# Prompt attention of a hybrid decoder layer: 64-query halves with 192 keys each, on parts of the TensorE array

## The chip, the core and the metric

The kernel runs on one core of one Trainium2 chip. The core has a matrix engine (TensorE, PE in the profile; its weight loads are listed apart as PEld), VectorE (DVE), ScalarE (ACT), GpSimd (POOL) and SyncE (SP), which here issues most transfers. Matrix products leave TensorE through PSUM, which has eight banks of 128 partitions by 512 fp32 values; DVE and ACT read them from there into SBUF, the working memory. The metric is device time of one execution in microseconds (us), as the median of several runs.

## What is computed

One decoder layer for a prompt of 1024 tokens and 8 sample sequences of 8 tokens: a gated feed-forward half step, a mixer, and a second feed-forward half step. The mixer has two head groups side by side: windowed attention and a gated linear recurrence (HGRN2). The change is in the attention of the prompt alone. It has 8 query heads of 64 columns, two key heads (each serves four query heads), a window of 128 tokens, and one learned sink per head that takes part in the softmax:

```python
s = jnp.einsum('bnqhgd,bnkhd->bnhgqk', qb, kk) * SCALE     # blocks of 128 queries, 256 keys
dist = qi + W - kj
band = (dist >= 0) & (dist <= WINDOW)
...
m = jnp.maximum(jnp.max(s, axis=-1, keepdims=True), sk)
p = jnp.exp(s - m)
den = jnp.sum(p, axis=-1, keepdims=True) + jnp.exp(sk - m)
...
out = jnp.einsum('bnhgqk,bnkhd->bnqhgd', p, vv)
```

A block of 128 queries sees the 128 keys before it and its own 128. A query sees at most 129 of these 256, so about half of each score matrix is masked. The first 64 queries of a block see only keys 0 to 191 of its 256, the last 64 only keys 64 to 255.

## The kernel before

**Stages and order.** The 1024 prompt tokens and 64 sample tokens go through in three groups of 320, 384 and 384 columns (n = 0, 1, 2), with 2, 3 and 3 prompt blocks of 128 queries; group 0 also has the sample tokens. Dense products of the feed-forward and projection layers are made by `mm3` (L249 to L253): each weight is split into a high and a low part, and three products (high by high, high by low, low by high) are added in one bank. These three lines are most of what TensorE does. The mixer is written as Python generators. `mixer(n)` (L1528) runs two chains in turn through `both`: one with `intra` and `hgrn_block`, one with `attn_block`. Each `yield` ends a step; `tick()` between dense products lets a stream go on by a rate given per group (`RM`, 0.97, 0.92 and 1.2 steps a tick). So the small products of the attention are strewn among dense ones. `need("m2")` (L1688) and the like run what is left of a stream at once.

A planner then walks the traced instructions with a simulated clock. It gives each tile a free buffer of its tag and puts the instructions of each engine in an order of its own: an instruction that is not ready there is overtaken by later ones that are. Each engine runs its list strictly in that order. Tags that matter here: `ax` (L65), four PSUM banks shared by all small products, and `t2` (L279), eight SBUF buffers of 512 columns. The dense products have four banks of their own.

**The attention of one block** (`attn_block`, L1185). Two passes, `pr` = 0 and 1, take four heads each: `g` is the key head, `i` the head within the pass.

- *Scores* (L1202): for each `i` and `g`, one product of 64 rows (the head's columns; key head `g` lies on partitions 64g to 64g+63) by 128 queries, with 256 keys streamed through. Each `g` writes its own bank. In the first block of the prompt there are 128 keys.
- *Softmax* (L1210 to L1222): DVE adds the mask `amask` and takes the row maximum in one instruction per head; small instructions merge it with the sink; ACT takes the exponential with a row sum per head. Two yields follow.
- *Transposes* (L1230): per `g` a bank with four 128 by 128 transposes of probabilities, then a copy to SBUF (L1233), by DVE for g = 0 and ACT for g = 1. One yield.
- *Values* (L1241): for each of two key blocks and each `g`, one product of 128 keys by 64 value columns, with 256 columns (two heads of 128 queries) streamed. Both `g` go to one bank `ob`, on its two halves of partitions, and this bank is kept over both passes. The scores of the second pass follow without a yield.
- After both passes: one copy of `ob` to SBUF (L1248), four transposes (`pvT`, L1252), division by the row sum, `finish_attn`.

A product of fp32 operands shows as two matmul records in the trace, a transpose as one.

`mix_consts` (L145) makes `amask` once, while the first feed-forward runs: a memset and two selections on GpSimd give a 128 by 256 band.

## Time and profile before

| quantity | value |
|---|---|
| median of 3 runs | 1960.29 us (1959.91 to 1961.1) |
| profiled execution, its own time | 1960.04 us |
| its span, first to last instruction | 1958.3 us |
| granted TensorE clock, mean | 0.999 |
| PE busy | 1945.1 us |
| DVE, ACT, POOL busy | 1431.4, 948.3, 171.9 us |
| transfers | 375.23 MB, mean 192 GB/s |

The span is that of the profiled execution; its own time has 1.7 us more around the span. Busy times of matmuls overlap: a matmul record lasts from its issue to its modelled end, and the next starts long before that. What a group of matmuls takes is therefore read from the starts: from its first start to the start of what follows on the same engine. In the groups, a form such as 64*128 stands for the rows and columns of the array that a product occupies; the shape behind it is the streamed operand. The prompt attention lies between 724 and 1304 us of the span.

### The profile page before, as it was taken

Reading aid. Unit: us, or ns where it says so; the run is one execution under the profiler, and the core shown is the slowest. Engines: PE = TensorE matmul, PEld = TensorE weight load, DVE = VectorE, ACT = ScalarE, POOL = GpSimd, SP = SyncE. Lnnn points to the kernel's source line nnn. Section 1 sums busy time; section 2 is a strip of 40 time slices with the busy share of each in tenths; the row PEclk is TensorE's granted clock in tenths of the full one; section 3 lists DMA queues with packets and bytes.
Section 4 is the critical chain, followed back from the end, with each engine's and each line's share of the span. In section 5 each row is a group of like instructions: output and inputs, shape, how many; then the busy total and the mean of one; then the engine's idle time right before and its main releaser. Section 6 shows DMA issues by size and latency. Waiting matters only on the chain.

```text
span 1958.3 us, 33735 instructions
## 1 busy us (share of the span) xinstructions
PE 1945.1 (99%) x13071; PEld 1817.2 (93%) x13071; DVE 1431.4 (73%) x2471; ACT 948.3 (48%) x1689; POOL 171.9 (9%) x161
## 2 busy tenths in 40 slices
PE   9999999999999999999999999999999999999998
PEld 9999999999998988778999898989999999999887
DVE  6896789886567656777677757756987887656666
ACT  5553444444445444435345545765644444445453
POOL 1300000000003102111121303000000000000202
PEclk9999999999999999999999999999999999999999
DMA  6643667655667547764424344536555645677974
GB/s 246 208 139 121 226 232 262 222 193 186 233 229 235 177 137 247 258 206 150 119 90 151 98 136 131 162 123 222 167 203 197 211 171 190 212 237 230 309 258 141
DMA packets 175601, 375.23 MB, mean 192 GB/s; under 512 B 16128, under 2 KB 67520, under 8 KB 175424
## 3 DMA queue, kind: packets, MB, share of 16 engines
q1 hardware_dynamic: 169536, 362.58, 55.2%
q10 hardware_dynamic: 5904, 10.49, 1.6%
q8 instruction: 102, 1.67, 0.3%
q14 instruction: 59, 0.48, 0.1%
HBM read 290.60 MB, written 83.39 MB: 191 GB/s over the span
## 4 chain that ended last, share of the span: by engine, by line
PE 91%; DVE 3%; DMA 3%; issue 1%; POOL 1%; ACT 1%; SPq 0%; DVEq 0%; POOLq 0%; ACTq 0%
PE mm L251 27%; PE mm L252 27%; PE mm L253 27%; DMA raw<-in_ffn_w_gu_dram 1%; PE sc L1202 1%; PE pv L1241 1%; PE pT L1230 1%; PE lv L1288 1%; DVE w L232 1%; DMA fa<-big 0%; PE c L253 0%; PE c L251 0%; PE c L252 0%; DVE t L751 0%; PE av L1375 0%
## 5 line engine op out<-in xcount | busy, mean ns | idle before, releaser
L251 PE MATMUL mm<-h,wsph 128*128 128x320 f32 (+1 forms) x1344 | 428.4, 320 | 0.0
L252 PE MATMUL mm<-h,wsph 128*128 128x320 f32 (+1 forms) x1344 | 425.6, 317 | 0.0
L253 PE MATMUL mm<-h,wspl 128*128 128x320 f32 (+1 forms) x1344 | 423.3, 316 | 0.0
L232 DVE TENSOR_TENSOR wspl<-raw,wsph 128x1024 fp32r<-128x1024 f32 x208 | 259.8, 1249 | 131.5 <-ACT wsph L231 130.1
L231 ACT CAST wsph<-raw 128x1024 fp32r<-128x1024 f32 x208 | 217.9, 1049 | 272.2 <-PE mm L252 215.1
L251 PEld LDWEIGHTS mm<-h,wsph 128*128 128x128 f32 x1344 | 252.3, 188 | 8.6 <-issue 6.7
L252 PEld LDWEIGHTS mm<-h,wsph 128*128 128x128 f32 x1344 | 252.6, 188 | 4.6 <-issue 3.8
L253 PEld LDWEIGHTS mm<-h,wspl 128*128 128x128 f32 x1344 | 252.0, 188 | 0.7 <-issue 0.4
L231 ACT CAST w<-raw 128x512 fp32r<-128x512 f32 (+1 forms) x208 | 153.8, 745 | 200.3 <-PE mm L252 90.0
L251 PE MATMUL mm<-h,w 128*128 128x384 f32 (+1 forms) x736 | 246.4, 335 | 1.0 <-ACT big L802 0.6
L252 PE MATMUL mm<-h,w 128*128 128x384 f32 (+1 forms) x736 | 245.9, 334 | 0.0
L253 PE MATMUL mm<-h,w 128*128 128x384 f32 (+1 forms) x736 | 240.6, 334 | 0.4 <-POOL w L604 0.4
L232 DVE TENSOR_TENSOR w<-raw,w 128x512 fp32r<-128x512 f32 (+1 forms) x208 | 178.3, 862 | 71.9 <-ACT w L231 71.2
L252 PE MATMUL mm<-w,h 128*128 128x512 f32 x462 | 180.8, 391 | 0.5 <-DVE w L232 0.5
L251 PE MATMUL mm<-w,h 128*128 128x512 f32 x462 | 180.3, 393 | 0.0
L253 PE MATMUL mm<-w,h 128*128 128x512 f32 x462 | 180.2, 392 | 0.0
L251 PE MATMUL mm<-big,w 128*128 128x384 f32 x528 | 176.7, 335 | 0.1
L252 PE MATMUL mm<-big,w 128*128 128x384 f32 x528 | 176.6, 334 | 0.0
L253 PE MATMUL mm<-big,w 128*128 128x384 f32 x528 | 176.0, 334 | 0.0
L251 PEld LDWEIGHTS mm<-h,w 128*128 128x128 f32 x736 | 138.3, 188 | 2.3 <-ACT big L802 1.3
L252 PEld LDWEIGHTS mm<-h,w 128*128 128x128 f32 x736 | 138.2, 188 | 0.4 <-DVE h L613 0.2
L253 PEld LDWEIGHTS mm<-h,w 128*128 128x128 f32 x736 | 137.8, 188 | 0.9 <-POOL w L604 0.6
(338 smaller groups left out, 3380.6 us busy)
## 6 DMA issues: line engine op xcount, KB each, us to landing
raw<-in_ffn_w_gu_dram SPq DMA_DIRECT2D x162, 512.0 KB
raw<-in_ffn_w_down_dram SPq DMA_DIRECT2D x74, 512.0 KB
raw<-in_w_in_dram SPq DMA_DIRECT2D x54, 512.0 KB
ar<-fa SPq DMA_DIRECT2D x70, 384.0 KB
big<-in_ffn_w_down_dram SPq DMA_DIRECT2D x88, 256.0 KB
fb<-big SPq DMA_DIRECT2D x44, 512.0 KB
fa<-big SPq DMA_DIRECT2D x22, 768.0 KB
raw<-fb SPq DMA_DIRECT2D x30, 512.0 KB
```

The costliest lines, as they stand in the source:

```text
L231: made['S'] = S.copy(hi, src).ins
L232: (lo_eng or V).tensor_tensor(lo, src, hi.bitcast(F32), op=ALU.subtract)
L251: PE.matmul(out, a[0], b[0], start=first, stop=False, skip_group_check=resume)
L252: PE.matmul(out, a[0], b[1], start=False, stop=False, skip_group_check=resume)
L253: return PE.matmul(out, a[1], b[0], start=False, stop=last, skip_group_check=resume).ins
L1202: PE.matmul(banks[g][:, i * 256:i * 256 + wk], zq[64 * g:64 * g + 64, 2 * pr + i, b * P:(b + 1) * P], kx[64 * g:64 * g + 64, k0:k0 + wk], ...
L1230: PE.transpose(bank[:, (kb * 2 + i) * P:(kb * 2 + i + 1) * P], pt[g][:, i, kb * P:(kb + 1) * P], ident)
L1241: PE.matmul(ob[64 * g:64 * g + 64, pr * 256:pr * 256 + 256], vn[:, vb, 64 * g:64 * g + 64], pT[g][:, kb * 256:kb * 256 + 256], start=kb == ...
L1288: PE.matmul(b5[32 * i:32 * i + 32, b, a], K[:, a, cs], Q[:, a, cs], start=True, stop=True)
```

## The change

The block of 128 queries is cut into two halves `hq` of 64 queries with 192 keys each.

- *Mask*: `amask` becomes 128 by 192. The band is made in a temporary tile; the upper half of the partitions copies its columns 0 to 191, the lower half columns 64 to 255.
- *Scores*: eight products per pass in place of four, each 64 rows by 64 columns of the array, with 192 keys streamed. `g` chooses the rows of the array, `hq` the columns. Queries of half `hq` land on partitions 64 hq to 64 hq + 63.
- *Softmax*: the same instructions over 192 columns. In the first block, where the halves have 64 and 128 keys, each instruction becomes two.
- *Probability tile*: it takes the middle 384 columns of a 512-column tile, and GpSimd zeroes 64 by 64 values at two corners (two memsets per `g`), so that every transpose can read 128 columns.
- *Transposes*: sixteen per pass in place of eight, each of 64 queries by 128 columns, on one 64-row half of the array; half `hq` writes its own bank. Still two copies of 512 columns, now one for each `hq`.
- *Values*: twelve products per pass in place of four, each 64 keys by 64 value columns, with 128 columns streamed. The row half of the array (`par`) chooses one of two banks; the order of work is three turns of four products.
- *Eviction of the values*: per pass, ACT copies one bank to SBUF and DVE adds the other, in place of one copy per block. The SBUF tile `of_` is taken at the start of the block.

```diff
--- before.py
+++ after.py
@@ -39,6 +39,7 @@
 LEVELS = [64, 32, 16, 8, 4, 2, 1]
 NRAW = 3
 WARM = 12
+PLACE = ((0, 0, 1), (1, 0, 0))
 P1 = 1.0
 
 
@@ -128,7 +129,7 @@
     f1pre = cp.tile([P, KC], F32, name="f1pre")
     halfpost = cp.tile([P, 16], F32, name="halfpost")
     sinkb = cp.tile([P, 8], F32, name="sinkb")
-    amask = cp.tile([P, 256], F32, name="amask")
+    amask = cp.tile([P, 192], F32, name="amask")
     smask = cp.tile([P, 136], F32, name="smask")
     ssink = cp.tile([P, 2], F32, name="ssink")
     seqm = cp.tile([NS, 4], F32, name="seqm")
@@ -146,11 +147,14 @@
         nc.sync.dma_start(sinkb, A["attn_sinks"].partition_broadcast(P))
         nc.sync.dma_start(ssink, A["sample_sinks"])
 
-        V.memset(amask, 0.0)
-        G.affine_select(amask, amask, pattern=[[1, 256]], compare_op=ALU.is_ge, fill=NEG,
+        band = tmp2("band", (P, 256))
+        V.memset(band, 0.0)
+        G.affine_select(band, band, pattern=[[1, 256]], compare_op=ALU.is_ge, fill=NEG,
                         base=0, channel_multiplier=-1)
-        G.affine_select(amask, amask, pattern=[[-1, 256]], compare_op=ALU.is_ge, fill=NEG,
+        G.affine_select(band, band, pattern=[[-1, 256]], compare_op=ALU.is_ge, fill=NEG,
                         base=P, channel_multiplier=1)
+        V.tensor_copy(amask[0:64], band[0:64, 0:192])
+        V.tensor_copy(amask[64:P], band[64:P, 64:256])
         tmp = pp.tile([P, 8, P], I32, tag="big", bufs=12, name="mtmp")
         tf = pp.tile([P, 8, P], F32, tag="big", bufs=12, name="mtmpf")
         col, row, x = tmp[:, 0], tmp[:, 1], tmp[:, 2]
         def attn_block(n, b):
             zq, kx, vn = Z[n]["q"], KX[n], VN[n]
             first = n == 0 and b == 0
-            nk = 1 if first else 2
-            k0 = P if first else b * P
-            wk = nk * P
-            mask = amask[:, P:] if first else amask
             sm, mx = small(), small()
-            ob = None
+            of_ = t2()
+            halves = (0, 1)
 
             def of(x, pr):
                 return x.rearrange("p (g r i) -> p g r i", g=2, r=2)[:, :, pr]
 
+            def cols_of(hq):
+                return slice((128, 64)[hq] if first else 0, 192)
+
+            def rows(par):
+                return slice(64 * par, 64 * par + 64)
+
             for pr in range(2):
-                pt, banks = [], [axbank("sc") for _ in range(2)]
+                pt, banks = [], [axbank("sc")[:, :384].rearrange("p (i c) -> p i c", i=2) for _ in range(2)]
                 for i in range(2):
-                    for g in range(2):
-                        PE.matmul(banks[g][:, i * 256:i * 256 + wk],
-                                  zq[64 * g:64 * g + 64, 2 * pr + i, b * P:(b + 1) * P],
-                                  kx[64 * g:64 * g + 64, k0:k0 + wk], start=True, stop=True)
+                    for hq in halves:
+                        cs = cols_of(hq)
+                        k0 = b * P + 64 * hq
+                        for g in range(2):
+                            PE.matmul(banks[g][rows(hq), i, cs],
+                                      zq[rows(g), 2 * pr + i, b * P + 64 * hq:b * P + 64 * hq + 64],
+                                      kx[rows(g), k0 + cs.start:k0 + cs.stop], start=True, stop=True)
+                parts = [(rows(hq), cols_of(hq)) for hq in halves] if first else [(slice(0, P), slice(0, 192))]
                 for g in range(2):
-                    p = t2((P, 2, 256))
-                    pt.append(p)
+                    pad = t2()
+                    p = pad[:, 64:448].rearrange("p (i c) -> p i c", i=2)
+                    pt.append((p, pad))
+                    G.memset(pad[rows(0), 448:], 0.0)
+                    G.memset(pad[rows(1), :64], 0.0)
                     for i in range(2):
                         hd = 4 * g + 2 * pr + i
-                        V.tensor_tensor_reduce(out=p[:, i, :wk], in0=banks[g][:, i * 256:i * 256 + wk], in1=mask,
-                                               op0=ALU.add, op1=ALU.max, scale=1.0, scalar=NEG,
-                                               accum_out=mx[:, 0, hd:hd + 1])
+                        for rs, cs in parts:
+                            V.tensor_tensor_reduce(out=p[rs, i, cs], in0=banks[g][rs, i, cs], in1=amask[rs, cs],
+                                                   op0=ALU.add, op1=ALU.max, scale=1.0, scalar=NEG,
+                                                   accum_out=mx[rs, 0, hd:hd + 1])
                 V.scalar_tensor_tensor(of(sm[:, 0], pr), of(mx[:, 0], pr), 0.125, of(sinkb, pr),
                                        op0=ALU.mult, op1=ALU.max)
                 V.tensor_scalar(of(sm[:, 1], pr), of(sm[:, 0], pr), -1.0, None, op0=ALU.mult)
                 for g in range(2):
                     for i in range(2):
                         hd = 4 * g + 2 * pr + i
-                        S.activation(pt[g][:, i, :wk], pt[g][:, i, :wk], AF.Exp, bias=sm[:, 1, hd:hd + 1],
-                                     scale=0.125, accum_out=mx[:, 1, hd:hd + 1])
+                        for rs, cs in parts:
+                            S.activation(pt[g][0][rs, i, cs], pt[g][0][rs, i, cs], AF.Exp, bias=sm[rs, 1, hd:hd + 1],
+                                         scale=0.125, accum_out=mx[rs, 1, hd:hd + 1])
                 V.tensor_tensor(of(sm[:, 2], pr), of(sinkb, pr), of(sm[:, 0], pr), op=ALU.subtract)
                 S.activation(of(sm[:, 2], pr), of(sm[:, 2], pr), AF.Exp)
                 yield
                 yield
-                pT = []
+                pT, tb2 = [], [axbank("pT").rearrange("p (g i s q) -> p g i s q", g=2, i=2, s=2) for _ in range(2)]
                 for g in range(2):
-                    bank = axbank("pT")
-                    for kb in range(nk):
-                        for i in range(2):
-                            PE.transpose(bank[:, (kb * 2 + i) * P:(kb * 2 + i + 1) * P],
-                                         pt[g][:, i, kb * P:(kb + 1) * P], ident)
-                    t = t2()
-                    (S.copy if g else V.tensor_copy)(t[:, :2 * wk], bank[:, :2 * wk])
+                    for i in range(2):
+                        for slot, at in ((0, (0, 64)), (1, (128, -64))):
+                            for hq in halves:
+                                if not first or at[hq] >= cols_of(hq).start:
+                                    c = 64 + 192 * i + at[hq]
+                                    PE.transpose(tb2[hq][:, g, i, slot], pt[g][1][rows(hq), c:c + P],
+                                                 ident[rows(hq), rows(hq)])
+                for hq in halves:
+                    t = t2((P, 2, 2, 2, 64))
+                    ss = slice(1 - hq, 2 - hq) if first else slice(0, 2)
+                    (S.copy if hq else V.tensor_copy)(t[:, :, :, ss], tb2[hq][:, :, :, ss])
                     pT.append(t)
                 yield
-                if ob is None:
-                    ob = axbank("pv")
-                for kb in range(nk):
-                    vb = b + kb + (1 if first else 0)
+                ob = [axbank("pv")[:, :256].rearrange("p (i h q) -> p i h q", i=2, h=2) for _ in range(2)]
+                for turn in (((0, 0), (0, 1)), ((0, 2), (1, 0)), ((1, 1), (1, 2))):
                     for g in range(2):
-                        PE.matmul(ob[64 * g:64 * g + 64, pr * 256:pr * 256 + 256], vn[:, vb, 64 * g:64 * g + 64],
-                                  pT[g][:, kb * 256:kb * 256 + 256], start=kb == 0, stop=kb == nk - 1)
+                        for par, (hq, blk) in enumerate(turn):
+                            if 64 * blk >= cols_of(hq).start:
+                                alone = (hq, blk) in ((0, 1), (1, 1))
+                                PE.matmul(ob[par][rows(g), :, hq], vn[rows(par), b + (blk + hq) // 2, rows(g)],
+                                          pT[hq][rows(par), g, :, PLACE[hq][blk]],
+                                          start=alone or first or blk == 0, stop=alone or blk == 2)
+                src = of_[:, pr * 256:pr * 256 + 256].rearrange("p (i h q) -> p i h q", i=2, h=2)
+                if first:
+                    S.copy(src[:, :, 0], ob[0][:, :, 0])
+                    V.tensor_copy(src[:, :, 1], ob[0][:, :, 1])
+                    V.tensor_tensor(src[:, :, 1], ob[1][:, :, 1], src[:, :, 1], op=ALU.add)
+                else:
+                    S.copy(src, ob[0])
+                    V.tensor_tensor(src, ob[1], src, op=ALU.add)
                 if pr:
                     yield
             V.tensor_tensor(mx[:, 2], mx[:, 1], sm[:, 2], op=ALU.add)
             V.reciprocal(mx[:, 3], mx[:, 2])
-            of_ = t2()
-            S.copy(of_, ob)
             yield
             tb = axbank("pvT")
             for m in range(4):
```

## Prediction

> **What bounds the kernel now.** I read the engine totals and the chain of waits first, then the groups by form, then the timeline of TensorE around single groups.
>
> ```profile
> PE 1945.1 (99%) x13071; PEld 1817.2 (93%) x13071; DVE 1431.4 (73%) x2471; ACT 948.3 (48%) x1689; POOL 171.9 (9%) x161
> ...
> PE 91%; DVE 3%; DMA 3%; issue 1%; POOL 1%; ACT 1%; SPq 0%; DVEq 0%; POOLq 0%; ACTq 0%
> ```
>
> TensorE is never free for long and 91% of the chain lies on it. A microsecond of its queue saved is therefore about a microsecond of the end, as long as no new wait on it appears. The three groups of prompt attention, by form:
>
> ```profile
> L1202 PE MATMUL sc<-kx,big 64*128 64x256 f32 x112 | 21.8, 404 | 0.0
> L1241 PE MATMUL pv<-t,vn 128*64 128x256 f32 x120 | 19.7, 395 | 0.0
> L1230 PE MATMUL pT<-ident,t 128*128 128x128 f32 x120 | 18.5, 276 | 0.8 <-ACT t L1219 0.8
> ```
>
> There are 16 passes (8 blocks, 2 each), 14 of them with 256 keys. Eight score records, eight value records and eight transposes make a pass. Busy times overlap, so what a pass takes is read from starts:
>
> ```profile
> 1290.16 0.31 PE L253 MATMUL mm<-h,wspl 128*128 128x320 f32 x1
> 1290.40 0.65 PE L1241 MATMUL pv<-t,vn 128*64 128x256 f32 x2
> 1290.97 1.14 PE L1202 MATMUL sc<-kx,big 64*128 64x256 f32 x8
> 1292.04 1.08 PE L1241 MATMUL pv<-t,vn 128*64 128x256 f32 x6
> 1293.05 0.41 PE L251 MATMUL mm<-h,wsph 128*128 128x320 f32 x1
> 1293.30 0.31 PE L252 MATMUL mm<-h,wsph 128*128 128x320 f32 x1
> ...
> 724.33 0.72 PE L1202 MATMUL sc<-kx,big 64*128 64x128 f32 x8
> 724.97 0.50 PE L251 MATMUL mm<-w,h 128*128 128x512 f32 x1
> ```
>
> Eight score records take 1.07 us with 256 keys (1290.97 to 1292.04) and 0.64 with 128. Two records run at once, one per key head: eight records are four rounds. So 128 streamed columns cost (1.07 - 0.64)/4 = 0.105 us a round, 256 cost 0.21, and 0.22 of the 1.07 is fixed: the first weight load, not hidden, and a gap after. Two value records (one product alone, two rounds) take 0.57, so their fixed part is 0.15.
>
> A stay of TensorE in a form other than 128*128 also delays the dense products on either side. The best row is an isolated stay of transposes in half the array, in the sample tokens:
>
> ```profile
> 903.93 0.33 PE L252 MATMUL mm<-h,wsph 128*128 128x384 f32 x1
> 904.10 0.34 PE L253 MATMUL mm<-h,wspl 128*128 128x384 f32 x1
> 904.37 0.46 PE L1350 MATMUL hT<-ident,t 64*128 64x64 f32 x4
> 904.76 0.45 PE L251 MATMUL mm<-h,wsph 128*128 128x384 f32 x1
> 905.04 0.34 PE L252 MATMUL mm<-h,wsph 128*128 128x384 f32 x1
> ...
> 1041.01 1.04 PE L1230 MATMUL pT<-ident,t 128*128 128x128 f32 x8
> 1041.88 0.60 PE L1367 MATMUL kT<-ident,big 128*128 128x128 f32 x4
> ```
>
> From 904.10 to 905.04 are 0.94 us, of which two dense products are 0.34 (904.10 less 903.93, twice). The four transposes and the stay cost 0.60. Today's transposes stay in the dense form and take 0.87/8 = 0.109 us each for 128 columns. Half the columns at the same rate give 0.055; with a little issue I take 0.06. The stay itself then costs 0.60 - 0.24 = 0.36 us.
>
> **The change part by part.** First, do four parts of the array run at once? Two do (above). The nearest row for four is the sample scores, 64*32, four column parts reading the same 64 rows:
>
> ```profile
> 850.31 0.44 PE L1421 MATMUL ssc<-big,t 64*32 64x136 f32 x8
> 850.67 0.45 PE L252 MATMUL mm<-h,wsph 128*128 128x384 f32 x1
> ```
>
> Eight records in 0.36 us: two rounds of 136 columns are 0.22, the rest is the fixed part. So four column parts run together, and row parts do so in the scores of before; four parts of two by two are not in this trace. I take them as concurrent.
>
> The Trainium skill speaks against it (TensorEngine Tiling (Array Packing), Instruction Overhead): each matmul carries about 60 cycles, and no factor should be taken out of a dimension that is already small. Scores, values and transposes go from 24 to 56 records a pass, and 32 more at 60 cycles of 2.4 GHz would by that estimate add 0.8 us a pass, 12 us in all, so the sum below would turn to a loss. The trace disagrees with it at the row above: there the second to fourth record of a round add nothing that shows.
>
> *Scores.* A pass goes from 4 rounds of 0.21 to 4 of 0.16 (192 columns), 0.84 to 0.63. Not all passes pair: in four of them the key heads come apart, each alone with four rounds:
>
> ```profile
> 1025.30 1.13 PE L1202 MATMUL sc<-kx,big 64*128 64x256 f32 x4
> 1026.35 0.45 PE L251 MATMUL mm<-h,wsph 128*128 128x384 f32 x1
> ...
> 1031.42 1.13 PE L1202 MATMUL sc<-kx,big 64*128 64x256 f32 x4
> ```
>
> There one key head takes the 1.05 us of a whole pass. After the change such a half still has its two query halves to pair: 0.84 to 0.63 each. Gain: 10 paired passes x 0.21 + 4 split x 0.42 = 3.8 us; the first block keeps its rounds (its second half has 128 keys). Weights of 64 columns in place of 128 cut the fixed part from 0.22 to the 0.15 of the values; over some 20 stays about 1.2 us. Scores: -5.0.
>
> *Values.* Four rounds of 0.21 become three turns of two rounds at 0.105, 0.84 to 0.63: 14 x 0.21 = -2.9.
>
> *No change of form between values and scores.* Both are 64 by 64 now. In the rows at 1290 the three groups carry fixed parts of 0.15, 0.22 and 0.17 in one row; one such part is left. A join saves about 0.19. The timeline has 13 joins: -2.5. If the second pass's scores no longer follow at once, this is lost (bound 0).
>
> *Transposes.* From 120 of 0.109 (13.1 us) to 240 of 64 columns: 16 in each of 14 passes and 8 in each of the first block's two. In pairs on the two row halves, which have a bank each: 120 x 0.06 = 7.2, gain 5.9; unpaired 14.4, a loss of 1.3. But they leave the dense form, so each stay costs 0.36, and they come in pieces:
>
> ```profile
> 1287.22 0.27 PE L1230 MATMUL pT<-ident,t 128*128 128x128 f32 x1
> ...
> 1287.78 0.49 PE L1230 MATMUL pT<-ident,t 128*128 128x128 f32 x3
> 1288.02 0.40 PE L251 MATMUL mm<-h,wsph 128*128 128x320 f32 x1
> 1288.26 0.27 PE L1230 MATMUL pT<-ident,t 128*128 128x128 f32 x1
> ...
> 1288.66 0.49 PE L1230 MATMUL pT<-ident,t 128*128 128x128 f32 x3
> ```
>
> The planner fits dense products between them, which is free today. I count 29 such pieces over the 16 passes; 16 is the least, 64 the most (one per head and pass): 5.8 to 23.0 us. The value bank is no longer held through the second pass's transposes, which frees one of four `ax` banks there, so I take 25 pieces: 9.0. Transposes: +3.1.
>
> *Banks.* Values need two `ax` banks for a short while; with two for the next scores all four are taken, and any bank held by the recurrence splits those scores. A new split costs 0.63 + 0.36 = 1.0 us. Bounds 0 and 8 splits; I take two: +2.0, since `u` and `av` have given theirs back in most of these steps.
>
> *DVE, ACT, POOL.*
>
> ```profile
> L1210 DVE CUSTOM_DVE_ANT_0 t<-sc,amask 128x256 f32<-128x256 f32 x56 | 20.7, 419 | 5.8 <-PE sc L1202 5.7
> L1210 DVE CUSTOM_DVE_ANT_0 t<-sc,amask 128x128 f32<-128x128 f32 x8 | 1.8, 281 | 0.0
> L794 DVE TENSOR_TENSOR big<-mm,big 128x384 f32<-128x384 f32 x44 | 24.4, 555 | 38.4 <-PE mm L253 38.4
> L1219 ACT ACTIVATE t<-t,sm 128x256 f32<-128x256 f32 x56 | 27.8, 499 | 25.2 <-DVE sm L1215 18.8 <-DVE sm L1221 6.3
> L1219 ACT ACTIVATE t<-t,sm 128x128 f32<-128x128 f32 x8 | 3.1, 391 | 0.0
> L1248 ACT COPY t<-pv 128x512 f32<-128x512 f32 x8 | 4.7, 583 | 0.2
> L1233 ACT COPY t<-pT 128x256 f32<-128x256 f32 x2 | 0.7, 365 | 0.0
> L1081 POOL MEMSET own<- 128x128 f32 x1 | 0.2, 205 | 0.0
> 700.00:1320.00 620.00, 617.05 (x5350) 539.25 (x5349) 434.14 (x921) 314.37 (x640) 94.06 (x83) 1.00 0.48 155
> ```
>
> At 192 columns a mask-and-maximum is about 0.35 us, an exponential 0.445. DVE: 56 x -0.07 = -3.9, 16 additions of at most 0.5 = +8. ACT: 56 x -0.054 = -3.0, copies 16 x 0.365 against 8 x 0.583 = +1.2. In the first block eight more of each kind add some 2 and 3 us. Against 434 and 314 busy of 620 us (the last row: PE, PEld, DVE, ACT, POOL), this lies beside TensorE. The addition on DVE waits for ACT's copy of the other bank, and behind it in DVE's order stand the next mask instructions and the weight splits of L232; eight buffers of split weights (`wsp`) give the products cover for that. Without it, each pass would show one copy, 16 x 0.365 = 5.8 us. 64 memsets on POOL (under 0.2 us each) lie there too; but the transposes wait for them, behind POOL's strict order, and behind the transposes stand dense products. Bound 0 to 1.5; I take 0.5. The new mask is made while feed-forward products run; no transfers are added or moved.
>
> *The last block* has little cover. Its wait shows as
>
> ```profile
> 1302.92 0.66 PE L1252 MATMUL pvT<-ident,t 128*128 128x128 f32 x4 [0.68 <-ACT t L1248]
> ```
>
> A copy of 0.365 and an addition of 0.5 stand where a copy of 0.583 did: +0.3.
>
> Sum: -5.0 - 2.9 - 2.5 + 3.1 + 2.0 + 0.5 + 0.3 = -4.5 us. The profiled execution took 1960.04 (span 1958.3 and 1.7 around it), 0.25 under the median; less 4.5 it is 1955.5, and 1955.8 beside the median. I say 1955.8.
>
> **Rivals.**
>
> *Transposes come apart (slower).* If exponentials arrive one by one when TensorE is ready, each head gets its own stay: up to 64 of 0.36. For it: the rows at 1287, where they come 1, 3, 1, 3. Against: eight in one row at 1041. From 25 to 64 stays is +14.0: 1969.8. It decides from 25 + 8.4/0.36 = 48 stays on (8.4 us is the way from the forecast to 0.2% above before).
>
> *Two parts at once, not four (slower).* Scores then take 8 rounds of 0.16, 1.26 us a paired pass in place of 0.63, and values 12 of 0.105, also 1.26 for 0.63: over the forecast 10 x 0.63 + 14 x 0.63 = 15.1, and 0.8 in the first block: 1971.7. It decides from about half of this on. For it: two by two is nowhere in the trace. Against: the four parts at 850.
>
> *Transposes in the row halves do not pair (no change).* +7.2: 1963.0. For it: no two such transposes stand side by side here. Against: the scores of the two key heads do pair on the same row halves.
>
> *Gain eaten by splits (no change).* Six more split scores: +6, 1961.8. For it: four of 14 passes split already. Against: the freed bank.
>
> **How the numbers follow.** A measurement of this kernel can tell 0.2% (3.9 us) from no change. Forecast, faster by more than that: 0.50. Transposes come apart beyond 48 stays: 0.13; four parts fail: 0.10. Unpaired transposes 0.10, splits and smaller mixtures 0.17, both within 0.2%. So faster 0.50, same 0.27, slower 0.23. Low end: 16 stays (-3.2) and no split (-2.0) and no other wait: 1950. High end, leaving out the upper part of the two slow rivals: 1966. The forecast's own range is 1950 to 1956.4.
>
> **What would show it.** Right: scores and values as one stay of some 1.5 us where they join; four records within about 0.03 us; transposes two by two at 0.06; about 25 stays of transposes. Wrong: rounds of scores that start 0.16 apart for every two records; transposes evenly spaced; many single pieces of four; new TensorE idle time before `pT` ended by POOL, or before `sc` by the addition on DVE.

## The result and the profile after

| kernel | median | lowest to highest | runs |
|---|---|---|---|
| before | 1960.58 us | 1959.91 to 1961.12 | 6 |
| after | 1966.68 us | 1961.82 to 1969.12 | 6 |

The ratio is 1.003, with a 95% interval of 1.0017 to 1.0043. That is a loss of 6.1 us, where 4.5 us of gain were predicted. It lies beyond the bound of 0.2% that the prediction used, though the lower end of the interval is just inside that bound. The runs of after also spread over 7 us, those of before over 1.2. The profiled execution of after took 1969.12 us (span 1967.4), the longest of its six, so its stages add up to more than the medians differ.

Engine totals and the chain of waits of after:

```profile
PE 1942.1 (99%) x13559; PEld 1817.4 (92%) x13559; DVE 1433.7 (73%) x2507; ACT 949.6 (48%) x1713; POOL 182.7 (9%) x225
...
PE 88%; DMA 4%; DVE 4%; ACT 2%; issue 1%; POOL 0%; SPq 0%; ACTq 0%; DVEq 0%; POOLq 0%
```

TensorE's busy time fell by 3 us, and yet the span grew. The chain shows where to look: TensorE's part fell from 91 to 88%, and DMA, DVE and ACT took it over. The dense products are the same 10242 records in both kernels, in nearly the same order (in after 66 places hold another product than in before), so the start of the n-th can be compared. The columns give by how many us it starts later than in before (minus: earlier), in the profiled execution of each kernel; the experiments behind the other columns are told below. "Merged first" is the changed kernel with the first block's instructions merged and the mask made on POOL; "tile" means that one tile has moved to other buffers.

```
start in     after   before   merged   merged,  group 0  group 0 old,
before, us           doubled  first    tile     old      tile
   313.9      2.0      2.0     2.8      0.7      0.1      1.5
   733.3      3.4      2.2     4.0      1.3      1.2      1.1
   763.6      8.6      6.3     3.8      1.1      1.2      1.4
   858.6     11.9     12.8     3.7      3.6      1.2      1.4
  1035.2     13.2     13.3     3.4      2.5      0.5      0.6
  1132.2     10.7     13.3     0.3     -2.5     -1.1     -4.6
  1293.6      7.7     13.2    -2.6     -8.2     -4.0    -10.2
  1316.4      9.1     13.2    -1.2     -5.8     -2.6     -7.9
  1941.6      9.1     13.2    -1.1     -5.4     -2.6     -7.8
```

After loses 8.5 us between 733 and 859 us, the first block and what follows on it, and gains 5.5 us between 1035 and 1294, where the attention of the later blocks lies. A difference of 2 us in the first row means little: four kernels of the experiments that run the same dense products as before up to 724 us start this one 1.2 to 2.0 us late as well.

The timeline of TensorE in after shows the new products as they were predicted:

```profile
1058.72 0.34 PE L255 MATMUL mm<-h,wsph 128*128 128x384 f32 x1
1058.99 0.89 PE L1262 MATMUL pv<-t,vn 64*64 64x128 f32 x24
1059.70 0.83 PE L1212 MATMUL sc<-kx,big 64*64 64x192 f32 x16
1060.46 0.44 PE L256 MATMUL mm<-h,wsph 128*128 128x384 f32 x1
...
1307.13 0.78 PE L1248 MATMUL pT<-ident,t 64*128 64x64 f32 x16
1307.85 0.42 PE L255 MATMUL mm<-h,wsph 128*128 128x320 f32 x1
```

Twenty-four value records take 0.71 us and sixteen score records 0.76, one behind the other, 1.47 us for the joined stay. Four parts of the array do run at once: in the trace the four records of a round start within 0.02 us, and the rounds 0.16 us apart. Sixteen transposes take 0.72 us with their stay, and two of them, one on each row half, 0.06.

### The profile page after: what moved, and what is told of

It reads as the page before. It is cut to its first block, busy times and chain, and to the rows that moved or that the text cites. A ratio compares the mean times of both kernels' runs of the same rounds, so it can differ in the third digit from the quotient of the medians.

```text
span 1967.4 us, 34910 instructions
## 1 busy us (share of the span) xinstructions
PE 1942.1 (99%) x13559; PEld 1817.4 (92%) x13559; DVE 1433.7 (73%) x2507; ACT 949.6 (48%) x1713; POOL 182.7 (9%) x225
## 4 chain that ended last, share of the span: by engine, by line
PE 88%; DMA 4%; DVE 4%; ACT 2%; issue 1%; POOL 0%; SPq 0%; ACTq 0%; DVEq 0%; POOLq 0%
PE mm L255 27%; PE mm L256 27%; PE mm L257 27%; DMA ar<-fa 1%; DMA raw<-in_ffn_w_gu_dram 1%; PE sc L1212 1%; ACT t L1235 1%; PE lv L1316 1%; DMA fb<-big 0%; PE pv L1262 0%; PE c L255 0%; PE c L257 0%; PE c L256 0%; DMA fa<-big 0%; PE pT L1248 0%
```

## What happens in the first block

The timeline of SP's queue, ACT and DVE in before, around the first pass of the first block. The columns are start, length, engine, line, operation and operands, and in brackets the idle time before it and what ended it:

```profile
725.58 0.37 SPq L974 DMA_DIRECT2D raw<-in_ffn_w_down_dram  x1
729.38 0.41 ACT L1219 ACTIVATE t<-t,sm 128x128 f32<-128x128 f32 x1
730.94 0.19 ACT L1222 ACTIVATE sm<-sm 128x4 f32<-128x4 f32 x1
731.03 1.04 ACT L231 CAST w<-raw 128x1024 fp32r<-128x1024 f32 x1
732.10 1.23 DVE L232 TENSOR_TENSOR w<-raw,w 128x1024 fp32r<-128x1024 f32 x1 [0.76 <-ACT w L231]
733.36 0.37 SPq L974 DMA_DIRECT2D raw<-in_ffn_w_down_dram  x1
```

And in after:

```profile
727.91 0.37 SPq L978 DMA_DIRECT2D raw<-in_ffn_w_down_dram  x1
733.78 0.35 ACT L1235 ACTIVATE t<-t,sm 64x64 f32<-64x64 f32 x1
737.13 0.40 ACT L1235 ACTIVATE t<-t,sm 64x128 f32<-64x128 f32 x1
737.65 0.21 ACT L1238 ACTIVATE sm<-sm 128x4 f32<-128x4 f32 x1
737.76 1.03 ACT L235 CAST w<-raw 128x1024 fp32r<-128x1024 f32 x1
738.82 1.23 DVE L236 TENSOR_TENSOR w<-raw,w 128x1024 fp32r<-128x1024 f32 x1 [6.36 <-ACT w L235]
740.08 0.37 SPq L978 DMA_DIRECT2D raw<-in_ffn_w_down_dram  x1
```

This is a loop: a weight lands, ACT makes its high part, DVE its low part, which frees the buffer, and then SP sends for the next weight. The activations of these products (`ar`, split into `h`) go round the same engines. In ACT's order the exponentials of the first block stand in the middle of this loop. They took 1.56 us in the first pass of before (729.38 to 730.94) and take 3.87 in after (733.78 to 737.65). They also start later, 6.0 us behind the start of the first maximum and not 3.9: the maxima on DVE are doubled, and other DVE work stands behind them. So DVE sat idle for 6.36 us, and from one weight transfer to the next went 12.2 us in place of 7.8. Stretches of before, and then the first of them in after (columns: busy time of PE, PEld, DVE, ACT, POOL with instruction counts, TensorE clock, DMA share, GB/s):

```profile
735.00:745.00 10.00, 10.00 (x129) 7.79 (x129) 7.08 (x12) 4.82 (x8) 3.59 (x2) 1.00 0.56 184
755.00:765.00 10.00, 10.00 (x94) 7.84 (x83) 5.19 (x7) 3.45 (x7) 5.36 (x6) 1.00 0.81 263
775.00:785.00 10.00, 10.00 (x51) 8.14 (x50) 6.95 (x26) 5.19 (x18) 0.00 (x0) 1.00 0.96 330
```

```profile
735.00:745.00 10.00, 10.00 (x217) 7.98 (x216) 4.82 (x7) 5.63 (x17) 2.17 (x2) 1.00 0.32 100
```

Transfers fell from 184 to 100 GB/s in this stretch, where TensorE still had work in store; over the 60 us from 725 to 785 the mean fell from 233 to 195. In before the transfers were busy at shares of 0.81 and 0.96 soon after, so there was little room to make this up. The chain of waits shows what it led to. Between 725 and 815 us all its large parts are TensorE's in before; in after the largest single part, 14.7%, is the transfer of activations, `ar<-fa`. The second pass of after pays again, and there TensorE itself waits:

```profile
744.69 0.60 PE L1212 MATMUL sc<-kx,big 64*64 64x64 f32 x8
750.37 0.65 PE L1212 MATMUL sc<-kx,big 64*64 64x64 f32 x8
755.88 0.21 DVE L1225 CUSTOM_DVE_ANT_0 t<-sc,amask 64x64 f32<-64x64 f32 x1
758.39 0.35 ACT L1235 ACTIVATE t<-t,sm 64x64 f32<-64x64 f32 x1 [2.86 <-DVE sm L1237]
760.36 0.28 PE L1248 MATMUL pT<-ident,t 64*128 64x64 f32 x2 [0.69 <-ACT t L1235]
761.32 0.27 PE L1248 MATMUL pT<-ident,t 64*128 64x64 f32 x2 [0.69 <-ACT t L1235]
762.29 0.28 PE L1248 MATMUL pT<-ident,t 64*128 64x64 f32 x2 [0.69 <-ACT t L1235]
...
763.30 0.39 PE L255 MATMUL mm<-w,h 128*128 128x512 f32 x1
763.77 0.63 PE L257 MATMUL mm<-w,h 128*128 128x512 f32 x1
```

The scores of the second key head come 5.7 us after those of the first, its maxima 5.5 us later still, and the transposes go out in four pairs, 0.96 us apart, each behind two exponentials. Right behind this wait a dense product of the same form takes 0.63 us where it took 0.39, and the starts lie 0.43 us apart where it was 0.23:

```profile
763.70:767.20 3.50, 3.50 (x10) 2.68 (x10) 3.21 (x6) 1.11 (x3) 1.93 (x2) 0.51 0.38 117
```

The granted clock is halved. The clock records of this trace hold one such stretch of 3.41 us here, one of 6.83 at 838.8 (it begins inside an idle time of TensorE of 2.8 us from 837.0 on) and one of 3.41 at 886.6: 13.65 us at half speed, so at most 6.8 us lost, in the longest of the six executions. A stretch at the very end of the span, 4.2 us here, is in every trace, that of before too.

## The experiments: undoing parts

Four kernels told the two visible edits of the first block and of the mask apart, and the place. All ratios below are to before on the same chip (1961.1 to 1961.4 us there), with the 95% interval; each kernel has 5 to 11 runs, beside 21 to 30 of before. The expectations count some 0.3 us more for a wait than the idle time that the profile shows; the text gives the idle time.

**First block merged.** Scores run over 128 keys for both halves, so that one instruction of 128 partitions does what two did:

```diff
-                        cs = cols_of(hq)
+                        cs = wide                     # slice(64 if first else 0, 192)
...
+        G.tensor_copy(fmask, amask[:, 64:192])
+        G.memset(fmask[0:64, 0:64], NEG)
...
+                G.memset(kx[:, 64:P], 0.0)
```

> Only the first block of the prompt is touched: its softmax runs over 128 columns on all 128 partitions at once (a mask of its own, 64 zeroed key columns), so its maxima and exponentials are 4 of each a pass and not 8 on half the partitions. Theory A (TensorE waits for the doubled exponentials of the first block; the halved clock behind it comes from that wait): the four transposes 963 ns apart at 759 us close up to one row, some 3 us are gained there directly, the clock is not halved at 764 us, together 5 us: about 1961.5. Rival B (the mask copies on DVE in the feed-forward are the loss): no change beyond 0.5 us, 1966.7. Rival C (the small products on parts of the array themselves bring the clock down, whatever TensorE waits for): up to 3 us from the wait, clock halvings stay, mean clock about 0.997: 1964.

Measured: 1959.77 us, 0.999 (0.9981 to 0.9998), below the 1961.5 of theory A. In the second pass there are four exponentials, and the spaced pairs are one row of eight transposes:

```profile
750.34 0.40 ACT L1240 ACTIVATE t<-t,sm 128x128 f32<-128x128 f32 x1 [0.70 <-DVE sm L1242]
758.30 0.46 PE L1253 MATMUL pT<-ident,t 64*128 64x64 f32 x8
```

No stretch of halved clock is left in group 0. Against its own before after lost 6.1 us, and this kernel gains 1.3: the edit is worth 7.4 us. With it the second key head's scores also come 1.4 us behind the first's, not 5.7, so the edit does not part the doubled instructions from the late scores; the next section does.

**Mask made on POOL.**

```diff
-        V.tensor_copy(amask[0:64], band[0:64, 0:192])
-        V.tensor_copy(amask[64:P], band[64:P, 64:256])
+        G.tensor_copy(amask[0:64], band[0:64, 0:192])
+        G.tensor_copy(amask[64:P], band[64:P, 64:256])
```

> Only the two copies that make the new mask go from DVE to POOL. Rival B: the two stalls of 1.7 us at 257 and 296 us of the span go back to those of before (0.9 and 1.1), 2.0 us are gained: 1964.7. Theory A and rival C: at 300 us of the span the difference to before is gone only as far as DVE's order is restored, and group 0 keeps its loss of some 11 us in a run with halved clock; time between 1964.5 and 1966.7.

Measured: 1967.81 us, 1.0029 (1.0018 to 1.004). The second of the two stalls is gone from its trace: an idle time of TensorE of 1.2 to 1.5 us at 298 to 300 us stands in all five traces whose mask is made on DVE, and at most 0.3 us in the others. The median shows nothing of it. Rival B falls as a cause of the result.

**Both.**

> Both edits: merged first block and mask copies on POOL. Theory A with B: all of the loss ahead of group 1 but the stall at 836 us goes, the gain of 6.3 us in groups 1 and 2 stays: 1956 to 1959, mean clock 0.999. Rival C: clock 0.996 to 0.998 still, 1961 to 1963.

Measured: 1958.96 us, 0.9988 (0.9979 to 0.9996), inside what theory A with B expected, and by the two runs before nearly all of it is owed to the merged block.

**Group 0 as before.** The old function for n = 0, the new one for the six blocks of groups 1 and 2:

```diff
-            at = [attn_block(n, b) for b in range(NPB[n])]
+            at = [(attn_block_old if n == 0 else attn_block)(n, b) for b in range(NPB[n])]
...
+            if (n, b) == (1, 0):
+                for c in (0, 64, 128):
+                    G.tensor_copy(amask[64:P, c:c + 64], amask[64:P, c + 64:c + 128])
```

> Group 0 (two blocks) has the attention and the mask of before; groups 1 and 2 (six blocks) have the new one, with the mask moved into its new form by three POOL copies of 64 columns between. Theory A (the loss lies in group 0, the PE work elsewhere is as costed): 1960.6 - 6.3 + 1.3 (last block) = 1955.6, clock 0.999. Rival C: the halved clock goes along with the new products into groups 1 and 2: 1959 or more, mean clock below 0.998. Rival D (the loss comes from a reshuffled order anywhere, not from group 0): the time does not come below 1960.

Measured: 1957.43 us, 0.9979 (0.997 to 0.9988), 1.8 us above theory A and below what C and D allow. The loss lies in group 0; where the new products run in groups 1 and 2 alone they gain. One stretch of halved clock stands in its trace all the same, at 1066 us, behind an idle time of 1.8 us.

## The experiments: which instructions, and why they cost so much

**The doubling alone, in before.** Nothing of the change but this:

```diff
+            parts = (slice(0, 64), slice(64, P)) if first else (slice(0, P),)
...
+                        for rs in parts:
+                            V.tensor_tensor_reduce(out=p[rs, i, :wk], in0=banks[g][rs, i * 256:i * 256 + wk], ...
...
+                        for rs in parts:
+                            S.activation(pt[g][rs, i, :wk], pt[g][rs, i, :wk], AF.Exp, ...
```

> The kernel before, with one thing of the change: in the first block of the prompt each maximum and each exponential is done in two instructions of 64 partitions. Theory A1 (the doubled instructions alone hold TensorE): the second pass's transposes wait for the exponentials, and the clock is halved behind that wait: 1963 to 1967, against 1961.1 without. Theory A2 (doubling hurts only together with the late scores of one key head, which the change has because its values take two banks): before, exponentials end at 750.4 us and the transposes start at 755.1, a slack of 4.7; doubling costs ACT 2.4 a pass and DVE 1.4, 3.8 in all, so it is hidden: 1960.5 to 1961.5.

Measured: 1971.88 us, 1.0053 (1.004 to 1.0065): 10.6 us, more than theory A1 had said, and my slack of 4.7 us was no cover at all. The same loop shows in its timeline. Some 12 us behind the exponentials of the second pass:

```profile
773.82 0.83 ACT L231 CAST h<-ar 128x768 fp32r<-128x768 f32 x1 [7.04 <-DMA ar<-fa]
774.69 0.96 DVE L232 TENSOR_TENSOR h<-ar,h 128x768 fp32r<-128x768 f32 x1 [6.31 <-ACT h L231]
```

and the windows around the two passes:

```profile
735.00:745.00 10.00, 9.19 (x137) 6.86 (x138) 4.56 (x7) 7.21 (x22) 1.58 (x1) 1.00 0.21 69
755.00:765.00 10.00, 9.49 (x103) 7.57 (x104) 6.39 (x13) 6.95 (x21) 1.44 (x2) 1.00 0.47 133
```

Against 184 and 263 GB/s of before in these two windows. ACT waits 7 us for data, while the transfers had been idle earlier: they were sent for too late. In the chain of waits between 725 and 815 us the transfer `ar<-fa` is now the largest part, with 24.5%, and the exponentials have 8.3%; TensorE's own idle times in this stretch, 7.4 us in all, are ended by DVE and ACT, in whose order these activations and the softmax stand. None of the new products is in this kernel, and it has a stretch of halved clock too, at 810 us, behind an idle time of 1.3 us. A halved clock needs none of the new products, and rival C falls.

**One of the two doublings.** The merged kernel with the exponentials doubled again, and with the maxima doubled again:

```diff
-                        S.activation(pt[g][0][:, i, wide], ...
+                        for rs in ((rows(0), rows(1)) if first else (slice(0, P),)):
+                            S.activation(pt[g][0][rs, i, wide], ...
```

> The changed kernel with merged maxima but doubled exponentials in the first block (as the run with the merged first block, 1959.8, but for the exponentials). If ACT's 2.4 us a pass are the cause, the waits of TensorE at some 759 us come back: 1964 to 1967. If the doubled maxima on DVE, or both together, are needed: 1959.5 to 1961.

> The other half: doubled maxima and merged exponentials in the first block. If ACT is the cause: 1959.5 to 1961. If the maxima (1.4 us a pass, and DVE's order behind them) are the cause: 1964 to 1967, with exponentials that start late, at some 758 us, though there are only four of them.

Measured: exponentials 1961.8 us, 1.0 (0.9991 to 1.0009), maxima 1968.59 us, 1.0033 (1.002 to 1.0045). I had expected ACT to weigh more; it is DVE. With the merged kernel at 1959.8 the exponentials cost 2.0 us, which is hardly clear of the noise, and the maxima 8.8. The parts do not add up: the maxima alone cost more than both doublings together in after (7.4). Every edit lets the planner lay out all engines anew, so that some of each difference may be the new order. In the trace with doubled maxima those of the second pass fall apart into two batches 4.4 us apart, with other DVE work between, and four exponentials wait for them:

```profile
749.62 0.27 DVE L1232 CUSTOM_DVE_ANT_0 t<-sc,fmask 64x128 f32<-64x128 f32 x1
754.00 0.27 DVE L1232 CUSTOM_DVE_ANT_0 t<-sc,fmask 64x128 f32<-64x128 f32 x1
757.63 0.40 ACT L1241 ACTIVATE t<-t,sm 128x128 f32<-128x128 f32 x1 [3.62 <-DVE sm L1243]
759.29 1.03 ACT L238 CAST w<-raw 128x1024 fp32r<-128x1024 f32 x1
761.75 1.82 SPq L244 DMA_DIRECT2D raw<-in_w_in_dram  x2
```

In the merged kernel the same four start at 750.3. Some 1.5 us of extra DVE time a pass thus become some 7 us for the exponentials, as other instructions take the places between, and the next weight's split and transfer stand behind them. In the chain of waits from 725 to 815 us the transfer `ar<-fa` has 35.0% here, and 4.5% in the kernel with doubled exponentials alone. That the order of the planner is what multiplies it is read from this trace; no run held the order fixed.

**The same doubling elsewhere.** `first` in the doubled kernel becomes `(n, b) == (1, 0)`.

> The kernel before, with the doubled maxima and exponentials of 64 partitions not in the first block of the prompt (that cost 10.6 us) but in the first block of group 1, where each runs over 256 keys and so costs DVE and ACT more than in the first block. Theory T (the 10.6 us come from the place: in the stretch from 725 to 815 us each weight's split on ACT and DVE, and so the next transfer on SP's queue, stands behind the softmax, and that stretch moves 184 to 330 GB/s; group 1 moves 120 to 130): at most 2 us, 1961 to 1963. Theory P (eight more instructions of 64 partitions cost this anywhere, as TensorE waits for the probabilities): 1970 or more.

Measured: 1964.59 us, 1.0015 (1.0006 to 1.0024): 3.2 us, above my 2 but far from 10.6. Its trace has two new waits of TensorE, 0.9 us each, for exponentials, and none for a transfer, and no transfer is among the larger parts of its chain from 960 to 1000 us. At this place such instructions cost about 3 us, as late probabilities. That the other 7 us in the first block belong to the place fits theory T, with a larger size than it gave.

**ACT work that the attention does not wait for.**

```diff
+                for k in range(12 if first else 0):
+                    S.activation(junk[:, :P], pt[k % 2][:, k // 2 % 2, :P], AF.Exp)
```

> The kernel before, with twelve exponentials of 128 by 128 that nobody uses, on ACT, in each of the two passes of the first block, behind the real exponentials. The attention waits for none of them; the next weight splits on ACT do, for some 4 us a pass. Theory T: the transfers that wait for these splits go out later, TensorE stalls on weights and activations: 1964 to 1969. Theory P (only late probabilities count): 1960.5 to 1961.5.

Measured: 1963.96 us, 1.0012 (1.0003 to 1.002): 2.6 us, at the low edge of theory T and outside theory P. Its two idle times of TensorE over 0.5 us in the first block, 0.9 and 0.6 us at 752, are not before a product of the attention, and `ar<-fa` has 10.0% of the chain from 725 to 815 us. Delayed splits of weights and activations alone do cost time.

## The experiments: the second loss

The table's column for the merged first block ends at -1.1 us, a smaller gain than predicted. A wait that after shares with it shows in the timeline of after in group 1:

```profile
1073.27 1.19 ACT L316 ACTIVATE sq<-big 128x320 f32<-128x320 f32 x3
1075.77 0.47 ACT L316 ACTIVATE sq<-big 128x320 f32<-128x320 f32 x1 [0.37 <-DVE ss L306]
1078.80 0.49 DVE L306 TENSOR_TENSOR ss<-ss,sq 128x320 f32<-128x320 f32 x1
1079.34 0.81 PE L290 MATMUL rb<-ss,omean 128*128 128x320 f32 x2 [2.06 <-DVE ss L306]
```

The norm of the next group squares its input in steps, each in one of the eight `t2` buffers, and DVE adds them up. In before four squares run in one row, and the broadcast product waits for nothing:

```profile
1060.44 1.56 ACT L312 ACTIVATE sq<-big 128x320 f32<-128x320 f32 x4
```

In after the fourth waits until DVE gives a buffer back, and TensorE stands for 2.06 us. The change takes its tile `of_` at the start of the block and not behind the second pass, so the attention holds a buffer more through both passes.

**The tile from the large buffers**, with group 0 as before, and with the merged first block:

```diff
-            of_ = t2()
+            of_ = big(F32, (P, 512))
```

> As the run with the attention of before in group 0 (1957.4), but the SBUF tile of the attention's values is taken from the twelve large buffers and not from the eight of 512 columns, which the squares of the next norm also use. If the wait of 2.1 us at 1064 us (the norm's broadcast product waits for sums of squares on DVE, whose squares on ACT come in pieces) is owed to these eight buffers: the wait goes, 1955 to 1956. If it is DVE's own order: 1957 to 1958.

> The same move of the tile, with the new attention in all blocks, the merged first block and the mask made on POOL (1959.0 without it). If the eight buffers cause the wait at 1067 us: 1956.5 to 1957.5, below the 1961.2 of before. If not: 1959.

Measured: 1952.23 us, 0.9954 (0.9941 to 0.9966), and 1954.63 us, 0.9962 (0.9949 to 0.9974): gains of 5.4 and 4.6 us (each pair taken against its own before), where some 2 were expected. In the trace of the first the four squares are one row again:

```profile
1061.73 1.55 ACT L313 ACTIVATE sq<-big 128x320 f32<-128x320 f32 x4
1064.57 0.81 PE L287 MATMUL rb<-ss,omean 128*128 128x320 f32 x2 [0.33 <-DVE ss L303]
```

and two other waits of TensorE, 0.9 us at 1208.6 and 0.6 at 1243.7, are gone too, with the stretch of halved clock at 1066. Both kernels beat before; the first is the fastest of this study.

**Is the shortage the change's own?** The same move in before, for all blocks of groups 1 and 2 but the middle one of group 1:

> The kernel before, with the tile of the attention's values taken from the large buffers in five of the six blocks of groups 1 and 2 (all but the middle block of group 1). Theory S (the shortage of 512-column buffers is the change's own: it holds the tile from the first pass on, and two buffers for probabilities beside it): no gain, 1960.5 to 1961.5. Theory W (before has the shortage too, and its waits at 1102 and 1210 us, 1.1 and 1.7 us, are part of it): 1957 to 1959.

Measured: 1961.6 us, 1.0 (0.9991 to 1.0008). Theory S holds: in these five blocks before has no such shortage.

**The tile alone in the changed kernel:**

> The changed kernel with this tile from the large buffers, and nothing else. If the two losses add up (7 to 8 us from the doubled maxima and exponentials of the first block, 4.3 to 5.2 from the buffers): 1966.7 - 4.8 = 1962, from 1961 to 1963. If they share a cause, or the tile also relieves the first block: below 1960.

Measured: 1960.68 us, 0.9999 (0.9991 to 1.0008), between the two readings: just under the 1961 to 1963 of losses that add up, and not below 1960. Against its own before the tile alone is worth 6.8 us, more than on the merged kernel (4.6). Eleven runs went from 1958.4 to 1966.0. The doubled first block with its waits and halved clock is still in its trace.

**Two more tests of place.** The last block of the prompt in the old form as well (on the kernel with group 0 as before), and only the first block in the old form, with the tile moved:

```diff
+ attn_block_old if n == 0 or (n, b) == (2, 2)
...
+ attn_block_old if n == 0 and b == 0
```

> As the run with the attention of before in group 0 (1957.4), and the last block of the prompt (the third of group 2) in the way of before too. If the last block's wait is owed to the transposes' banks by query half (both copies must wait for all sixteen transposes, where before the first copy could start after four), the 1.3 us lost there come back and a little PE gain goes (0.5 to 1): 1956 to 1957. If that wait has another cause, in ACT or DVE: 1957.5 to 1959.

> The first block of the prompt as before, all others new, the tile from the large buffers there. If the first block's softmax is all that the new attention loses in group 0: as the run with all of group 0 as before (1952.2) less the gain of one new block, 1951 to 1953. If the new second block of group 0 brings its own wait: 1953 to 1956.

Measured: 1957.98 us, 0.9982 (0.9973 to 0.9991), and 1954.97 us, 0.9969 (0.996 to 0.9978). The time of the first falls in the range for another cause. In its trace, however, the last block's wait before the values went, and the kernel had gained 1.6 us less before it (2.4 us at 1293.6 in place of 4.0), so the time stayed: I had put that gain too low. The run puts the whole old block in place of the new, so it does not tell the transposes' banks from the rest of the block. In after this wait reads:

```profile
1310.41 0.89 PE L1262 MATMUL pv<-t,vn 64*64 64x128 f32 x24 [1.42 <-DVE t L1253]
```

The second suggests that the second block of group 0 in its new form loses some 2.7 us (1954.97 against 1952.23), though the two intervals overlap. What makes it lose is open; its trace has idle times of TensorE of 1.5 us at 830 and of 1.3 at 836, with a halved clock from 840.9 on, that the other doesn't have.

## Why the prediction was wrong, point by point

- **Four parts at once, scores, values, joins: right.** The joined stay took 1.47 us (1.5 predicted). Scores of 16 records take 0.76 us for four rounds. In both kernels values and scores come in 30 stays; before changes form 13 times inside such a stay, after never.
- **Transposes: right, a little better.** They pair, and come in 19 stays (25 taken).
- **Bank splits: right.** Five of the 14 later passes have their key heads apart (four in before), and the first block's second pass is new: two, as taken. But the price of 1.0 us was that of TensorE alone. In the first block the split put the second key head's scores 5.7 us behind the first's; what that alone costs, no run shows.
- **The sum over TensorE: right or low.** With both losses removed the change gains 6.7 us (1954.63 against 1961.36) where 4.5 were predicted. This is a net figure; no run splits it into the terms of the sum.
- **The memsets on POOL: +0.5 taken, nothing seen.** No idle time of TensorE over 0.6 us between 700 and 1320 us of after is ended by POOL.
- **"In the first block eight more of each kind add some 2 and 3 us ... this lies beside TensorE": the step that failed.** In the first pass DVE's part grew by 1.3 us and ACT's by 2.3, so 2.6 and 4.6 for the two passes, where 2 and 3 were taken. Above all the cover was wrong. It was argued from 434 and 314 busy us of 620, an average over the whole attention. In the first block both engines stand in the loop that fetches weights and activations, and a delay there is a later transfer, and TensorE waits for late probabilities besides. Cost: 7.4 and 8.3 us (after against the two merged kernels, each from its own before).
- **The buffers: a term that is missing from the sum, and so was put at nothing.** The prediction counted PSUM banks and not the eight SBUF buffers, though the tile `of_` is taken earlier. Cost: 4.6, 5.4 and 6.8 us (the three pairs with and without the moved tile, each from its own before).
- **The last block: +0.3 taken, +1.4 measured** (from 1293.6 to 1316.4 us in the table). TensorE waits 1.4 us for the copies of the probabilities. A bank holds one query half of both key heads, so no copy can start before the last transposes; that this is the reason is read from the kernel and not tested alone.
- **The mask: taken at nothing.** About 1 us in the traces, at 298 to 300 us, not to be seen in the medians.
- **The rivals.** None named the cause. "Transposes come apart" decided nothing: in the first block's second pass they come in four pairs, as a consequence of the late exponentials, and two other passes have two and three pieces.

The two losses of about 8 and 5 us, against a gain of some 7, make the measured 6.1. This adds up by construction, since the gain is what is left when both are removed, and how the 13 us divide depends on the order: 8.3 and then 4.6 if the block is merged first, 6.8 and then 6.0 if the tile is moved first.

## What to carry to other kernels

An engine's mean load does not tell that an instruction is hidden: look, at the place itself, for what stands behind it in that engine's order, and follow it as far as the next transfer. Count every pool that a change draws on, SBUF buffers as well as PSUM banks, for the whole time that a tile is held. A special case at the edge (here the first of eight blocks) can cost more than the body gains; making it regular, with masked work, was the better trade here.

## What was not expected of the hardware

The granted TensorE clock fell to half in steps of 3.41 us. Between 700 and 1320 us the traces of the 17 kernels hold 16 such stretches, in ten of them and none in before. Twelve begin within some 4 us of an idle time of TensorE: a single one of 1.3 to 2.8 us, or the spaced transposes of the first block. Three of the other four lie at one place, 880 to 887 us. But of 37 single idle times of 1.3 us or more only nine have one beside them. What decides stays open. In the stretch shown above dense products start 0.43 us apart in place of 0.23, so that each stretch of 3.41 us costs about 1.6 (an estimate). The times of after spread over 7 us, with three stretches in its trace, and those of the fastest kernel over 0.8, with none. But only one execution of each kernel is traced, and four others whose trace has none between 700 and 1320 us (the last block old, the doubling in group 1, the extra ACT work, the tile moved in before) spread over 3.7 to 5.2 us.

An exponential with row sums on half the partitions was not cheaper but dearer. In the first pass of before one of 128 by 128 starts every 0.39 us; in after those of 64 by 64 and 64 by 128 are followed by the next after 0.45 and 0.52 us (pairs in 0.97). In the kernel with the doubling alone, those of 64 by 128 start 0.51 us apart, so that halving the partitions at the same columns makes ACT's time for the tile 1.03 us in place of 0.39.
